# The three passes of a split float32 product in another order

## The chip, the core and the metric

One core of one Trainium2 chip runs the whole program. The metric is the device time of an execution in microseconds; before the change three runs took 2352.8, 2357.6 and 2357.88 us, median 2357.6 us. What is asked is how the reordering of the passes moves this number.

## What is computed

Two blocks on 512 tokens of 1024 features. The first is a hybrid layer, the second a two-layer block with 256 further context tokens:

```python
def hybrid_layer(x, ...):
    h = rmsnorm(x, norm1_w)
    aq, ak, av, bq, bk, bv, br, ba, cq, ck, cv = jnp.split(h @ w_in, ...)
    mix = concat([dilated_attention(aq, ak, av), gla(bq, bk, bv, br, ba), moba_attention(cq, ck, cv)])
    x = x + mix @ w_out
    h2 = rmsnorm(x, norm2_w)
    return x + jnp.square(jax.nn.relu(h2 @ w_ff1)) @ w_ff2
```

The second block (two layers) modulates its norms by a condition vector, projects the input (1024 x 1696), runs latent attention with rotary keys over tokens and context, a Fourier mix and a long convolution, multiplies the mix by an output matrix, and closes each layer with a feed-forward of the same kind (1024 to 4096 and back). All of it is float32, and most of the work is products of a weight matrix with the tokens.

## The kernel before

TensorE takes its operands in the type float32r, which keeps fewer bits than float32. So that a product has float32 accuracy, each operand is split into a high part (the value rounded to float32r) and a low part (the rest), and the product is made of three matmuls into one PSUM bank: high weights on high data, low weights on high data, high weights on low data. `mm3` (L128 to L131) issues these three; in it `whi` and `wlo` are the stationary operand, `xhi` and `xlo` stream. Each matmul comes with a load of its stationary tile, which the profile shows on a row of its own (PEld).

Who makes the four operands: `load_w` (L109 to L119) brings a weight tile of 128 x 1024 by DMA on SP's queue into one of three buffers, ACT writes the high half (`whi`, L117), and DVE subtracts to get the low half (`wlo`, L118). Data are split in the same way by `split` (L133 to L143) or, in the feed-forward, by L261 (ACT, `uh`) and L262 (DVE, `ul`): high on ACT first, low on DVE after it.

Who calls `mm3`: the projections of the first block (`proj1`, 24 passes per weight tile of 128 output features: 8 blocks of 128 input features by three), the scores of its heads and of the second block's attention (there "weights" are the queries and "data" the keys), the projections of the second block (`front`), the heads' queries and keys, the output projections (`out_pieces`), and both halves of the three feed-forwards (`mlp`). The feed-forward goes in 8 groups of 4 hidden tiles: four products with `w1` (24 passes each), the activation on ACT and DVE, then 8 products with `w2` (12 passes each). Behind a norm the first three weight tiles go through one part of the tokens (256 columns) after the other, so that three products are open at once. `values` (L651 to L653), the first block's values (L978 to L980) and the filters (L429) write their three matmuls out by hand and do not use `mm3`.

Order: the program text hands instructions with priorities to a scheduler, which writes each engine's list at build. It takes from what its own estimate says is ready, earliest priority first; matmuls into one bank stay in their order. While the first block's feed-forward runs, work that does not depend on it (modulations, filters, the context's first layer) is handed in on a lane of its own and fills in between; its sums lie in the bank named `e`, the main work's mostly in `d`. From tile 28 of that feed-forward on, the scheduler works with a finer estimate: `timed.enter_context(tc.block(name="second", schedule_with_timeline_sim=True))`.

Of the kernel before, what the change touches and what calls it, by code (L numbers as in the profile page):

```python
# [18 lines left out]
DRAM = bass.MemoryType.DRAM  # L19
# [9 lines left out]
# the parts that the tokens of a stream (0: x, 1: context) are worked on in where a norm would hold up the rest  # L29
# [17 lines left out]
def kernel(ctx: ExitStack, tc: tile.TileContext, A, out, dbg=None):  # L47
# [36 lines left out]
    # ---------------------------------------------------------------- helpers  # L84

    # Buffers of one name are handed out in program order. Work that shall overtake other work needs its own: a lane.
# [34 lines left out]
    def after(cur, prev):  # L121
        """cur is issued behind prev on the same engine."""
        if prev is not None:
            tc.add_manual_dep(cur.ins, prev.ins.name, mybir.DependencyInfo(
                mybir.DependencyClass.NoSync, mybir.DependencyReason.DATA), reason="psum group order")
        return cur

    def mm3(ps, whi, wlo, xhi, xlo, start, stop):  # L128
        pe.matmul(ps, lhsT=whi, rhs=xhi, start=start, stop=False)  # L129
        pe.matmul(ps, lhsT=wlo, rhs=xhi, start=False, stop=False)  # L130
        pe.matmul(ps, lhsT=whi, rhs=xlo, start=False, stop=stop)  # L131

    def split(hi, lo, src, scale=None, shift=None):  # L133
        """hi + lo = src * scale + shift, each exact in float32r."""
# [16 lines left out]
    def rstd_steps(srcs, n, width, psum, name="n", parts=None, gains=None, ending=1):  # L151
        """In two pieces, the steps for the first sources and a call for the rest and the result:
        1 / sqrt(mean over features + eps), on every partition; srcs: [128, n] feature tiles. With parts: a list of
        calls, one per part of the tokens, that give it. With gains: of y = rms_norm(src) * gain, rms_norm(y) being
        src * gain times what the first such list gives, and y src * gain times what the second gives."""
# [18 lines left out]
        def rest():  # L174
            for sl in parts:
                for i in range(together, len(srcs)):
                    add(i, sl)
                if gains:
                    # 1 / (r1 r2)^2 = mean((x gain)^2) + eps / r1^2
# [26 lines left out]
    def normed(hT, srcs, rstd, scale, shift=None):  # L206
        """hT[k] (hi, lo) = srcs[k] * rstd * scale[k] (+ shift[k])"""
# [5 lines left out]
    def normed_stream(hT, v, psum, gain, shift, ending, rest=None):  # L213
        """normed for a whole stream, one part of its tokens after the other"""
# [5 lines left out]
    def by_parts(n_tiles, units, lead):  # L220
        """Order of work of weight tiles on units of tokens: the first tiles go through unit after unit, so that
        later units can still be on their way."""
# [3 lines left out]
    def mlp(streams, w1, w2, pool_u, psum, side=None, rstd=None, ending=1):  # L226
        """x[m] += gate(m) * (relu(h @ w1)^2 @ w2)[m] for each stream (x, hT, n, gate); h = hT (* rstd)"""
        parts = [PARTS[0 if st[2] == S else 1] for st in streams]
        for g in range(32 // GRP):
# [34 lines left out]
            # towards the end the tokens' parts come one after the other, for the norm behind  # L264
# [6 lines left out]
            for mb, mm, ci, sl in steps:  # L271
                if mb not in ws:
                    # the last weights have buffers of their own: the others are for what comes next
# [18 lines left out]
    # ---------------------------------------------------------------- residual streams  # L292
    # The first block needs its input for its first norm and again where it adds to it; in between, the memory
    # of the residual stream serves the modulations.
# [3 lines left out]
    # ---------------------------------------------------------------- work on the second block's weights alone  # L298
# [3 lines left out]
    def filling(behind=0):  # L302
        """Work for when nothing else is ready."""
# [5 lines left out]
    # shift1, norm1_g * (1 + scale1), gate1, shift2, norm2_g * (1 + scale2), gate2; one column per feature tile  # L309
# [5 lines left out]
    def modulations(held, passing, scratch, behind=None):  # L315
        """silu(c) @ w_mod + b_mod for both condition vectors, by products and sums along the free axis."""
# [42 lines left out]
    def filters(fp, psum, which):  # L359
        """Spectra of the long convolutions at the odd half frequencies, cosine and sine parts."""  # L360
# [78 lines left out]
    # ---------------------------------------------------------------- second block, one stream at a time  # L439
# [10 lines left out]
    def mixers(lq, n):  # L450
        """Fourier input, convolution gate, convolution input"""
        return [[lq.tile([128, n], F32, name=f"{nm}{i}") for i in range(2)] for nm in ("F", "x0_", "z")]

    def front_norm(pi, ps, l, v, rest=None):
        """Normed and modulated input."""
# [18 lines left out]
    def front(pi, ps, l, v, lat, mixin, hT):  # L474
        """The input's projections and their latents."""
# [13 lines left out]
        # the convolution's inputs come last: until then their tiles are free  # L489
# [35 lines left out]
        def conv(i, p, dst):  # L525
            """dst = short convolution of channel tile i along tokens"""
# [113 lines left out]
    def values(ap_, ps, l, key_lats):  # L640
        """Values of all heads, token-major."""
# [17 lines left out]
    def attention(ap_, sm, l, v, key_lats, lat, ps, es=None, lp=None, fill=()):  # L659
        """Latent attention of stream v over the keys of key_lats; its output, transposed, in four tiles, which may  # L660
        take the memory of the latents in lp. fill: pieces of other work on the tensor engine."""
# [5 lines left out]
        # the rotary rows of the keys are the same for every head  # L667
# [9 lines left out]
        def heads(j, ps):  # L677
            """queries and keys of a pair of heads"""
# [88 lines left out]
        # behind the rest of the attention in order: for when nothing of it is ready  # L767
# [6 lines left out]
    def out_half(l, half, src, v, ps):  # L774
        """x += gate * (four of the mix tiles) @ w_out"""
# [3 lines left out]
    def out_pieces(l, half, src, v, ending=4):  # L779
        """out_half in pieces, each with the pool of its sums' bank; those of the last weight tiles one part of the  # L780
        tokens after the other"""
# [26 lines left out]
    def side_lane(wrk, width=0, stage=0, split_=0, banks=3):  # L808
        """A lane of its own, with weight buffers where width is given."""
# [704 lines left out]
```

## Time and profile before

| what | value |
|---|---|
| median of three runs | 2357.6 us |
| the profiled execution: span from its first to its last instruction | 2353.3 us |
| TensorE matmul (PE) busy, matmuls | 2287.6 us, 12,907 |
| weight loads (PEld) busy | 1898.1 us |
| VectorE (DVE) busy | 1469.5 us |
| ScalarE (ACT) busy | 996.0 us |
| mean granted TensorE clock | 0.990 |

The profile comes from one execution; the profiled one's time as a run is not listed, only its span, which is 4.3 us below the median of the runs. PE's busy time counts a matmul from its start to a modelled end, and neighbours overlap, so the pace of passes is read from their starts, not from their lengths. `PEld` runs beside `PE`. A wait names what ended an engine's idle time. L-numbers are lines of the kernel.

### The profile page before, as it was taken

How to read it: one execution, taken by the hardware profiler on the slowest of the kernel's cores; microseconds unless marked ns; L12 is line 12 of the kernel's file. 1: busy time of each engine (PE TensorE's matmuls, PEld its weight loads, DVE VectorE, ACT ScalarE, POOL GpSimd, SP SyncE). 2: the span in 40 equal slices, each digit the busy share in tenths (PEclk: the TensorE clock that was granted, in tenths of full speed). 3: DMA queues.
4: the chain of work that ended last, by engine and by line, in shares of the span. 5: the costliest groups of instructions: out<-in, count | busy, mean ns of one | idle time of the engine just before them, and what ended most of it. 6: DMA issues, size and time to landing. Idle time of an engine off the chain costs nothing.

```text
span 2353.3 us, 32927 instructions
## 1 busy us (share of the span) xinstructions
PE 2287.6 (97%) x12907; PEld 1898.1 (81%) x12907; DVE 1469.5 (62%) x2641; ACT 996.0 (42%) x1717; POOL 137.0 (6%) x173
## 2 busy tenths in 40 slices
PE   8999999999999999899999999999899999999997
PEld 7866677778877788788988888888878788888886
DVE  7888778576666684766785554533755666443345
ACT  5344553344344452654533322343443644333333
POOL 0022200000000000321000000000001220000000
PEclk9999999999999999999999999999999999999999
DMA  6523454434331422102354442321222101332232
GB/s 232 166 76 131 130 166 151 164 134 141 126 100 63 149 82 72 54 19 75 106 180 152 152 152 72 103 90 59 83 89 73 41 28 46 107 99 98 90 99 72
DMA packets 78853, 248.52 MB, mean 106 GB/s; under 512 B 9342, under 2 KB 13872, under 8 KB 77930
## 3 DMA queue, kind: packets, MB, share of 16 engines
q1 hardware_dynamic: 78698, 246.42, 31.9%
q8 instruction: 102, 1.67, 0.3%
q14 instruction: 53, 0.43, 0.1%
HBM read 241.63 MB, written 4.75 MB: 105 GB/s over the span
## 4 chain that ended last, share of the span: by engine, by line
PE 87%; DVE 6%; DMA 3%; ACT 2%; issue 1%; POOL 0%; SPq 0%; DVEq 0%; ACTq 0%; POOLq 0%
PE d L129 23%; PE d L130 22%; PE d L131 22%; PE o L760 3%; PE t L750 2%; DVE wlo L118 1%; PE s L129 1%; PE s L131 1%; DMA area<-in_wmod_dram 1%; PE e L129 1%; PE s L130 1%; PE e L429 1%; PE o L1042 1%; PE e L130 1%; PE e L131 1%
## 5 line engine op out<-in xcount | busy, mean ns | idle before, releaser
L117 ACT ACTIVATE whi<-wstage 128x1024 fp32r<-128x1024 f32 (+4 forms) x318 | 324.6, 1024 | 511.0 <-PE d L131 426.3
L118 DVE TENSOR_TENSOR wlo<-wstage,whi 128x1024 fp32r<-128x1024 f32 (+4 forms) x318 | 378.0, 1191 | 256.2 <-ACT whi L117 253.5
L129 PE MATMUL d<-uh,whi 128*128 128x512 f32 (+1 forms) x1056 | 380.4, 361 | 1.3 <-ACT uh L261 1.3
L130 PE MATMUL d<-uh,wlo 128*128 128x512 f32 (+1 forms) x1056 | 379.8, 360 | 0.0
L131 PE MATMUL d<-ul,whi 128*128 128x512 f32 (+1 forms) x1056 | 374.3, 359 | 0.0
L129 PEld LDWEIGHTS d<-uh,whi 128*128 128x128 f32 x1056 | 198.5, 188 | 33.8 <-ACT uh L261 2.2
L131 PEld LDWEIGHTS d<-ul,whi 128*128 128x128 f32 x1056 | 198.9, 188 | 32.4 <-issue 1.5
L130 PEld LDWEIGHTS d<-uh,wlo 128*128 128x128 f32 x1056 | 198.7, 188 | 30.9 <-issue 1.3
L287 DVE SCALAR_TENSOR_TENSOR area<-d,mod,area 128x512 f32<-128x512 f32 (+1 forms) x134 | 95.4, 725 | 145.2 <-PE d L131 145.1
L256 ACT ACTIVATE w<-d 128x256 f32<-128x256 f32 (+1 forms) x96 | 50.4, 525 | 215.9 <-PE d L131 209.2
L338 DVE SCALAR_TENSOR_TENSOR w<-wm,cb 128x1024 bf16<-128x1024 f32 x96 | 114.9, 1220 | 25.7 <-DMA wm<-in_wmod_dram 25.5
L262 DVE TENSOR_TENSOR ul<-w,uh 128x512 fp32r<-128x512 f32 (+1 forms) x128 | 79.3, 622 | 19.9 <-ACT uh L261 19.8
L338 DVE SCALAR_TENSOR_TENSOR mj<-area,area 128x1024 bf16<-128x1024 f32 x64 | 79.7, 1246 | 6.9 <-DMA area<-in_wmod_dram 6.1
L739 DVE TENSOR_REDUCE mx<-s 128x1 f32<-128x768 f32 x64 | 61.2, 956 | 33.6 <-PE s L131 32.8
L260 ACT ACTIVATE w<-w 128x512 f32<-128x512 f32 (+1 forms) x128 | 73.0, 570 | 6.5 <-DVE w L258 5.6
L261 ACT ACTIVATE uh<-w 128x512 fp32r<-128x512 f32 (+1 forms) x128 | 73.9, 577 | 3.5
L744 POOL TENSOR_SCALAR sb<-sb,mx 128x768 f32<-128x768 f32 x64 | 57.9, 906 | 207.7 <-DVE mx L740 80.4
L760 PE MATMUL o<-pt,V 128*64 128x128 f32 x768 | 64.9, 281 | 0.0
L285 DVE TENSOR_TENSOR area<-d,area 128x512 f32<-128x512 f32 (+1 forms) x66 | 44.2, 672 | 31.4 <-PE d L131 31.1
L750 PE MATMUL t<-c_ident,sb 128*128 128x128 f32 x384 | 60.7, 281 | 0.8 <-ACT pt L753 0.7
L674 POOL CAST k000h<-kr0h 32x512 fp32r<-32x512 f32 x2 | 1.7, 844 | 1017.9 <-PE d L625 1017.9
L287 DVE SCALAR_TENSOR_TENSOR ctx<-d,mod,ctx 128x256 f32<-128x256 f32 x64 | 30.8, 481 | 48.0 <-PE d L131 47.8
(1185 smaller groups left out, 5761.0 us busy)
## 6 DMA issues: line engine op xcount, KB each, us to landing
wstage<-in_w_m_dram SPq DMA_DIRECT2D x128, 512.0 KB, 3.5
wstage<-in_w_ff_dram SPq DMA_DIRECT2D x64, 512.0 KB, 4.2
wm<-in_wmod_dram SPq DMA_DIRECT2D x64, 512.0 KB, 4.2
wstage<-in_w_in_dram SPq DMA_DIRECT2D x56, 512.0 KB, 3.4
area<-in_wmod_dram SPq DMA_DIRECT2D x32, 512.0 KB, 4.2
wstage<-in_w_out_dram SPq DMA_DIRECT2D x32, 512.0 KB, 3.5
wstage<-in_w_v_dram SPq DMA_DIRECT2D x8, 520.0 KB, 4.2
ktab<-in_kt_dram SPq DMA_DIRECT2D x16, 256.0 KB, 2.7
```

Of the source, the lines that this page charges most:

```text
L117: act.activation(hi[:, a:b], st[:, a:b], AF.Copy)
L118: dve.tensor_sub(lo[:, a:b], st[:, a:b], hi[:, a:b].bitcast(F32))
L129: pe.matmul(ps, lhsT=whi, rhs=xhi, start=start, stop=False)
L130: pe.matmul(ps, lhsT=wlo, rhs=xhi, start=False, stop=False)
L131: pe.matmul(ps, lhsT=whi, rhs=xlo, start=False, stop=stop)
L260: act.activation(u, r, AF.Square)
L261: act.activation(uh, u, AF.Copy)
L262: mark[g, j] = dve.tensor_sub(ul, u, uh.bitcast(F32))
L287: dve.scalar_tensor_tensor(x[m][:, sl], ps, gate(m), x[m][:, sl], op0=OP.mult, op1=OP.add)
L338: after(dve.scalar_tensor_tensor(t, w, 1.0, sv[v], op0=OP.mult, op1=OP.mult, accum_out=mraw[l][v][j // 8][:, j % 8:j % 8 + 1]), behind)
L750: pe.transpose(pt[:, (kk - a) * 128:(kk - a + 1) * 128], sb[:, kk * 128:(kk + 1) * 128], ident)
L760: last_[h2] = after(pe.matmul(po[64 * h2:64 * h2 + 64, q], lhsT=V[kk][:, 64 * h_:64 * h_ + 64], rhs=PT[h2][:, kk * 128:(kk + 1) * 128], st ...
```

## The change

The second and third pass of `mm3` change places. The rest of the diff takes away comments and descriptions, line for line, so that all line numbers stay.

```diff
     def mm3(ps, whi, wlo, xhi, xlo, start, stop):
         pe.matmul(ps, lhsT=whi, rhs=xhi, start=start, stop=False)
-        pe.matmul(ps, lhsT=wlo, rhs=xhi, start=False, stop=False)
-        pe.matmul(ps, lhsT=whi, rhs=xlo, start=False, stop=stop)
+        pe.matmul(ps, lhsT=whi, rhs=xlo, start=False, stop=False)
+        pe.matmul(ps, lhsT=wlo, rhs=xhi, start=False, stop=stop)
```

## Rows read from the trace of the kernel before

**Rows 1.** Page, part 1: busy time, share of the span, instructions, of each engine.

```profile
PE 2287.6 (97%) x12907; PEld 1898.1 (81%) x12907; DVE 1469.5 (62%) x2641; ACT 996.0 (42%) x1717; POOL 137.0 (6%) x173
```

**Rows 2.** Page, part 4: the chain that ended last, shares by engine.

```profile
PE 87%; DVE 6%; DMA 3%; ACT 2%; issue 1%; POOL 0%; SPq 0%; DVEq 0%; ACTq 0%; POOLq 0%
```

**Rows 3.** Page, part 5: groups; busy us, mean ns | idle before, releaser.

```profile
L117 ACT ACTIVATE whi<-wstage 128x1024 fp32r<-128x1024 f32 (+4 forms) x318 | 324.6, 1024 | 511.0 <-PE d L131 426.3
...
L118 DVE TENSOR_TENSOR wlo<-wstage,whi 128x1024 fp32r<-128x1024 f32 (+4 forms) x318 | 378.0, 1191 | 256.2 <-ACT whi L117 253.5
...
L129 PE MATMUL d<-uh,whi 128*128 128x512 f32 (+1 forms) x1056 | 380.4, 361 | 1.3 <-ACT uh L261 1.3
...
L130 PEld LDWEIGHTS d<-uh,wlo 128*128 128x128 f32 x1056 | 198.7, 188 | 30.9 <-issue 1.3
```

**Rows 4.** Busy time by stretch, PE: length, busy (matmuls), granted clock, DMA, GB/s; last layer.

```profile
2000.00:2100.00 100.00, 100.00 (x435) 1.00 0.33 106
2100.00:2200.00 100.00, 100.00 (x434) 1.00 0.29 95
```

**Rows 5.** Timeline, PE then PEld, 1796 us: start, us, instruction, tiles, shape, count.

```profile
1796.60 0.39 PE L651 MATMUL d<-whi,ckv00h 128*128 128x512 f32 x1
1796.83 0.40 PE L652 MATMUL d<-wlo,ckv00h 128*128 128x512 f32 x1
...
1796.37 0.19 PEld L651 LDWEIGHTS d<-whi,ckv00h 128*128 128x128 f32 x1
1796.61 0.19 PEld L652 LDWEIGHTS d<-wlo,ckv00h 128*128 128x128 f32 x1
```

**Rows 6.** Waits of PE: who, for whom, us in total, times, longest us.

```profile
PE d L130 <- DVE wlo L118: 1.0, 3, 0.4
```

**Rows 7.** Waits of PEld: the same columns.

```profile
PEld d L130 <- DVE wlo L118: 2.3, 4, 0.9
...
PEld e L130 <- DVE wlo L118: 1.2, 7, 0.3
```

**Rows 8.** Timeline, PE, the second weight tile of the start.

```profile
16.11 0.40 PE L129 MATMUL d<-mix0h,whi 128*128 128x512 f32 x1
16.95 0.50 PE L130 MATMUL d<-mix0h,wlo 128*128 128x512 f32 x1 [0.44 <-DVE wlo L118]
```

**Rows 9.** Timeline, PE, first product behind the norm of the first feed-forward.

```profile
313.16 0.28 PE L130 MATMUL d<-h0h,wlo 128*128 128x256 f32 x1
313.49 0.39 PE L131 MATMUL d<-h0l,whi 128*128 128x256 f32 x1
```

**Rows 10.** Timeline, PE, the first feed-forward's first passage from w1 to w2.

```profile
342.69 0.40 PE L129 MATMUL d<-uh,whi 128*128 128x512 f32 x1
343.04 0.50 PE L131 MATMUL d<-ul,whi 128*128 128x512 f32 x1
```

**Rows 11.** Timeline, PE, behind the context's norm in the second block.

```profile
1675.77 0.38 PE L129 MATMUL d<-h10h,whi 128*128 128x256 f32 x1 [0.24 <-ACT h10h L136]
...
1676.46 0.28 PE L130 MATMUL d<-h10h,wlo 128*64 128x256 f32 x1
1677.54 0.58 PE L131 MATMUL d<-h10l,whi 128*128 128x256 f32 x1 [0.81 <-DVE h10l L137]
...
1683.63 0.27 PE L129 MATMUL d<-h14h,whi 128*128 128x256 f32 x1
...
1685.48 0.28 PE L130 MATMUL d<-h15h,wlo 128*64 128x256 f32 x1
```

**Rows 12.** Timeline, DVE then PE, a passage from w1 to w2, last layer.

```profile
2052.09 0.69 DVE L262 TENSOR_TENSOR ul<-w,uh 128x512 fp32r<-128x512 f32 x1
...
2052.84 0.39 PE L130 MATMUL d<-uh,wlo 128*128 128x512 f32 x1
```

**Rows 13.** Stretch, PE, behind the wait of rows 11: the columns of rows 4.

```profile
1677.90:1683.40 5.50, 5.50 (x27) 0.50 0.00 0
```

## What I expect of the change, and why

> **What bounds the kernel now.** I read the page first. TensorE is busy for 2287.6 of 2353.3 us, the next engine (DVE) for 62% [rows 1], and the chain that ended last is PE for 87% of the span [rows 2]. The reader is to see there that PE's list of passes sets the time: only 65.7 us (2353.3 - 2287.6) are left in which PE has nothing running, and most of what a change can do off PE is hidden. The groups come next. One pass of `mm3` has a matmul and a weight load; the load takes 188 ns on its own row, beside the matmul that runs [rows 3]. ACT needs 1.02 us and DVE 1.19 us to split a weight tile in two, and both idle before it until PE has freed a buffer [rows 3]: on the whole weights wait for PE, not PE for weights. In the last layer 434 or 435 matmuls of 512 columns run in 100 us at full clock, so a pass costs 100/434 = 0.230 us [rows 4]; of 256 columns, 16 passes from 1683.63 to 1685.48 us take 1.85 us, 0.116 us each [rows 11]. Then I read the waits of PE and of its loads for the two operands that change places, the low weights and the low data [rows 6, 7], and last the timeline where each of them is made just in time [rows 8 to 12], and the clock behind the longest such hole [rows 13].
>
> **What the change does to a triple.** The first pass stays. The pass that reads the low data (`xhi`'s remainder) becomes the second, the pass that reads the low weights becomes the third. No pass, load, split or DMA is added or removed, and the sum in PSUM ends with the third pass as before, so whoever empties the bank waits for the same number of passes. What moves are four deadlines, each by one pass: low weights may come 0.230 us later (0.116 us at 256 columns), low data must come as much earlier; the high weights and the low data are let go one pass earlier, the low weights and the high data one pass later.
>
> **The passes themselves: 0, ends -5 and +5 us.** 12,907 matmuls [rows 1] before and after. Which tile streams while which one is loaded does change, and no row of before shows the new pairs in `mm3`. The spread between like stretches, 434 against 435 passes [rows 4], is 0.23%, about 5 us on the span; I keep it as the bound on both sides and take 0, because the nearest row with the new pairing is plain. In `values` the stationary tile is already used twice in a row (`ckv00h` in L651 and L652), and there the second pass starts 0.23 us after the first, like any other [rows 5].
>
> **The repeated high weights: 0.** After the change the first and second pass of each triple have the same stationary tile. In the same rows it is loaded again, 0.19 us at 1796.37 and 0.19 us at 1796.61 us [rows 5]: the second load is not left out, and it lies beside a running matmul either way. At 256 columns, where a load has less to hide behind, a pass still costs 0.116 us, half of the 0.230 us of 512 columns; so the loads do not set the pace there either, and leaving one out would win at most 0.0004 us on a third of 12,907 passes, 2 us. The Trainium skill, "TensorE: Matmul & The Clock Gate", Part 2, says that loading is decoupled from computing so that one can load once and matmul repeatedly, which speaks for this order. Here the trace does not agree that it happens by itself: the tile is loaded twice. By the rule one load in three would go; by the rows that gives 0 to 2 us, so the sum is the same.
>
> **Low weights later: -1.0 us, ends 0 and -1.8 us.** PE waits for `wlo` in the second pass 3 times, 1.0 us in all [rows 6]; its loads wait 4 times in the main stream (2.3 us) and 7 times in the filling work (1.2 us) [rows 7]. Each such wait can shrink by one pass at most: 4 x 0.230 + 7 x 0.116 = 1.7, rounded up to 1.8. An example is the second tile of the start: first pass at 16.11 us, second only at 16.95 us, because the low weights are late [rows 8]; now the low-data pass fits into that hole. Some of the seven lie in filling work for which something else stands ready, so I take 1.0.
>
> **Low data earlier: +1.5 us, ends +0.8 and +6.8 us.** This is where the change costs. Behind a norm or an activation the high half comes from ACT and the low half from DVE after it, and PE so far bridges that with the low-weight pass of every product that is open. Behind the norm of the first feed-forward two products are open, and PE waits from 313.16 + 0.12 to 313.49 us for `h0l` [rows 9]: two passes fewer to fill with, 2 x 0.116 = 0.23. Behind the context's norm three are open (six passes from 1675.77 us, the last at 1676.46), then PE stands until 1677.54 us for `h10l`, 0.81 us of it idle [rows 11]: 3 x 0.116 = 0.35. In the first passage from w1 to w2 two products are open and `ul` comes some 0.1 us late already (342.69 + 0.23 against 343.04) [rows 10]: one pass more, 0.23. The other 23 passages (8 groups in each of three feed-forwards, less this one) have room by the planner's order: in the last layer `ul` is done at 2052.09 + 0.69 = 2052.78 us, and the slot that will want it starts at 2052.84 [rows 12]. 0.06 us is little, but nothing is lost; I take 0 and keep 23 x 0.23 = 5.3 for the upper end. About five more norm edges and six head pairs make up a guess of 0.7 (five to six times one pass of 0.116). 0.23 + 0.35 + 0.23 + 0.7 = 1.5.
>
> **Releases: 0.** High weights freed a pass earlier and low weights a pass later: ACT splits first and DVE follows 1.02 us behind it [rows 3], so the later release of 0.23 us is not the last to come; if that cover went, it would cost 0.23 us where a tile is waited for, which is inside the ends above. SP's and POOL's queues have nothing moved past them.
>
> **The order that is written at build.** The program's list on each engine is laid out by a scheduler that takes what is ready by its own estimate. Its estimate of `wlo` and `ul` now falls in other slots, so pieces of filling work can land elsewhere. The trace cannot show the new list. The unit of such a mishap is one product, 24 passes x 0.230 = 5.5 us, put into a stretch where PE would idle, or taken out of one; I take 0 and let it make the rivals.
>
> **Sum.** -1.0 + 1.5 = +0.5 us. It is made against the profiled span, 2353.3 us; the median of the runs is 2357.6, so 4.3 us lie around the span, and I leave them as they are: 2357.6 + 0.5 = 2358.1 us. The direct ends alone are -1.0 (0.8 - 1.8) and +6.8; with the pass rate's 5 us they are 2351.6 and 2369.4 us.
>
> **Rivals.** (A) Slower: the low data become the late operand. Place: the passages from w1 to w2. If `ul` is not there at the second pass in all 24, they cost 5.3 us more than I count: 2363.4 us. It decides where the slack at today's third pass is under one pass, 0.23 us; for it speaks that the slack in rows 12 is 0.06 us after the change, against it that the scheduler has other banks open to fill with, as rows 10 show (another product's first pass at 342.69). A hole can also cost clock: behind that of rows 11 the granted clock is 0.50, the lower of the two levels (1.2 GHz), for 5.5 us with 27 passes [rows 13], 0.20 us each against 0.116 from 1683.63 on [rows 11]; 5.5 - 27 x 0.116 = 2.4 us. One more such stretch makes 2366. (B) Faster: the new list happens to put one or two products into today's 65.7 us without matmuls: -5.5 to -11 us, about 2350. For it speaks only that the idle time is there; against it that most of it lies at the start, at the norms and at the end, where nothing is ready. The same with the other sign, 2364 us or so, is as likely by itself. (C) Faster: the second load of the same tile does not happen after all; by the rows above 2 us at most, 2356, which is within the forecast. (D) The pairs of streamed and loaded tiles are better or worse by the whole spread of rows 4: 2353 or 2363.
>
> **How the numbers follow.** About 0.2%, 4.7 us, is what a measurement of this kernel can tell from no change. Forecast (with C): 0.51. Slower: A 0.19, the list 0.07, D 0.03, together 0.29. Faster: B 0.16, D 0.04, together 0.20. I take the range from 2348 to 2369 us: it holds the direct ends with the pass rate, one product won or two lost, and leaves out the rest of B and the worst of A with several slow-clock stretches.
>
> **What would show it.** Right: matmuls 12,907 and loads as many; passes of 0.230 us in the last layer; PE's waits for `wlo` nearly gone and waits for `ul`, `h..l` new, in the second pass; the wait for `h10l` near 1.2 instead of 0.81 us. The prediction is wrong if the pace of passes in the last layer differs from 434 in 100 us by more than one, if passages from w1 to w2 show PE idle in every group, or if the stretches with filling work end earlier or later by several microseconds with no wait that answers for it.

## The result, and the profile after

The changed kernel takes 2370.17 us (four runs, 2365.75 to 2373.19) against 2357.74 us: a ratio of 1.0053 [1.0038, 1.0067], or 12.4 us more. Measured once more beside other kernels it took 2369.99 us, 1.0052 [1.0035, 1.0069]. The prediction, 2358.1 us with a range up to 2369, was wrong: the change costs time, and it costs more than any rival had priced.

The page of the profile after (span 2363.7 us, mean granted clock 0.987), with the lines that answer to [rows 1 to 3]: part 1, the shares of the chain from part 4, groups of part 5.

```profile
PE 2296.7 (97%) x12907; PEld 1901.7 (80%) x12907; DVE 1472.8 (62%) x2641; ACT 1003.2 (42%) x1717; POOL 136.2 (6%) x173
...
PE 87%; DVE 6%; DMA 3%; ACT 2%; issue 1%; POOL 0%; SPq 0%; DVEq 0%; ACTq 0%; POOLq 0%
...
L117 ACT ACTIVATE whi<-wstage 128x1024 fp32r<-128x1024 f32 (+4 forms) x318 | 325.7, 1027 | 797.8 <-PE d L130 678.4
...
L130 PEld LDWEIGHTS d<-ul,whi 128*128 128x128 f32 x1056 | 198.9, 188 | 32.8 <-issue 1.7
...
L131 PEld LDWEIGHTS d<-uh,wlo 128*128 128x128 f32 x1056 | 198.5, 188 | 31.7 <-issue 1.7
```

The reader is to see that nothing in kind has changed: as many matmuls, as many loads, those of the feed-forwards at the same 188 ns, the same chain. L130 is now the pass of the low data, L131 that of the low weights. Nor does PE stand still much longer: its idle time was 2353.3 - 2287.6 = 65.7 us and is 2363.7 - 2296.7 = 67.0 us. Its busy time grew by 9.1 us, so the same passes took longer. What is different stands in three other views. First the pace in the last layer (busy time by stretch, PE: length, busy, matmuls, granted clock, DMA, GB/s), 432 where [rows 4] had 434:

```profile
2020.00:2120.00 100.00, 100.00 (x432) 1.00 0.30 95
2120.00:2220.00 100.00, 100.00 (x432) 1.00 0.30 96
```

Second PE's waits (who, for whom, us in total, times, longest us) and those of its loads; compare [rows 6, 7]:

```profile
PE t L1035 <- POOL sb L1032: 4.3, 5, 1.3
...
PE d L129 <- ACT h0h L139: 1.5, 1, 1.5
...
PE d L130 <- DVE h10l L137: 1.1, 1, 1.1
...
PE d L130 <- DVE h0l L140: 0.7, 1, 0.7
...
PE d L131 <- DVE wlo L118: 0.7, 2, 0.4
...
PE d L130 <- DVE h00l L137: 0.4, 1, 0.4
...
PE e L131 <- DVE wlo L118: 0.2, 1, 0.2
...
PEld e L131 <- DVE wlo L118: 2.2, 8, 0.4
...
PEld d L131 <- DVE wlo L118: 1.3, 2, 0.7
```

Between 85 and 335 us the trace of before has 3.2 us for the first of these lines and 0.8 for the second:

```profile
PE t L1035 <- POOL sb L1032: 3.2, 6, 1.0
...
PE d L129 <- ACT h0h L139: 0.8, 1, 0.8
```

Third, the granted clock behind these gaps (the columns of the first view), after and then before:

```profile
208.90:212.30 3.40, 2.17 (x12) 1.00 0.33 129
212.30:215.70 3.40, 3.40 (x11) 0.50 0.00 0
...
236.20:239.60 3.40, 2.32 (x10) 1.00 0.37 134
239.60:243.00 3.40, 3.40 (x11) 0.50 0.05 20
314.70:318.10 3.40, 1.39 (x9) 1.00 1.02 300
318.10:321.50 3.40, 3.40 (x18) 0.51 1.04 291
```

```profile
208.90:212.30 3.40, 3.40 (x27) 1.00 0.49 178
212.30:215.70 3.40, 3.24 (x18) 1.00 0.40 118
...
236.20:239.60 3.40, 2.40 (x11) 1.00 0.76 258
239.60:243.00 3.40, 3.40 (x20) 1.00 0.07 27
314.00:317.40 3.40, 3.40 (x30) 1.00 1.07 228
317.40:320.80 3.40, 3.40 (x26) 1.00 0.55 164
```

After the change PE stands still for 1.2 us at 209.6 and again at 236 (a transpose waits for the softmax that POOL finishes) and for 1.5 and 0.7 us at the norm of the first feed-forward, and behind each the granted clock is 0.50, the lower of its two levels (1.2 GHz). In the profile of before none of these three falls is there. A profile is one execution, so the falls from 200 to 330 us are counted over all traces of the runs below, without the two kernels that were filled in block 1 (here the first block up to its output projection). With the new order in block 1's head scores all six traces have one to three falls there. With the old order seven of eight have none. One, of the kernel with low weights first in the last feed-forward, has one at 237.7 us, behind a wait of 1.0 us at which the kernel before, with the same list of passes up to there, kept its clock.

To see where the time lies I take the ends of the same eight DVE instructions in each trace (the first `ul`, the 33rd and 64th maximum of L739, the 1st, 127th, 145th and 181st sum of L287, the end) and list how much longer each stretch is than in the profile of before. In brackets stands half of what its stretches at half clock are longer: the work that the clock withheld.

| us, from before | to 330 | to 1023 | to 1150 | to 1668 | to 1883 | to 2070 | to 2282 | to the end | sum |
|---|---|---|---|---|---|---|---|---|---|
| changed | +5.1 (+5.1) | +0.8 | +1.1 | +0.3 | -0.2 (+1.7) | +2.0 (+1.7) | +1.3 | 0.0 | +10.4 (+8.6) |
| changed, again | +12.7 (+13.7) | 0.0 | +1.0 | +0.3 | -0.2 (+1.7) | +1.9 (+1.7) | +1.3 | 0.0 | +17.0 (+17.1) |

Two things can be read. The large, varying part lies before 330 us, and there it is the size of the lost clock. A steadier part of 4 to 5 us lies behind it, 1.3 us of it in 212 us of the last feed-forward where PE never waits and the clock is 1.00. The Trainium skill, "TensorE: Matmul & The Clock Gate", Terms, prices time at the half clock at one half of it. Up to 330 us the two traces agree (5.1 for 5.1, 12.7 for 13.7); later the price is lower. From 283 us on two kernels of the last section, with block 1's heads or its projections taken back, have the changed kernel's list of passes. From 1668 to 1883 us these four traces took -1.3, -0.2, -0.2 and +1.0 us against before, with 0, 1.7, 1.7 and 3.4 us of work withheld: 2.3 us for 3.4, about two thirds.

### The profile page after: what moved, and what is told of

Read it like the earlier page. It is cut to its first block, busy times and chain, and to the rows that moved or that the text cites. A ratio compares the mean times of both kernels' runs of the same rounds, so it can differ in the third digit from the quotient of the medians.

```text
span 2363.7 us, 32973 instructions
## 1 busy us (share of the span) xinstructions
PE 2296.7 (97%) x12907; PEld 1901.7 (80%) x12907; DVE 1472.8 (62%) x2641; ACT 1003.2 (42%) x1717; POOL 136.2 (6%) x173
## 4 chain that ended last, share of the span: by engine, by line
PE 87%; DVE 6%; DMA 3%; ACT 2%; issue 1%; POOL 0%; SPq 0%; DVEq 0%; ACTq 0%; POOLq 0%
PE d L130 22%; PE d L129 22%; PE d L131 22%; PE o L760 3%; PE t L750 2%; DVE wlo L118 1%; PE s L129 1%; PE s L131 1%; PE s L130 1%; PE e L129 1%; DMA area<-in_wmod_dram 1%; PE o L1042 1%; PE e L131 1%; PE e L130 1%; ACT whi L117 1%
## 5 line engine op out<-in xcount | busy, mean ns | idle before, releaser
L130 PE MATMUL d<-ul,whi 128*128 128x512 f32 (+1 forms) x1056 | 378.8, 360 | 0.0
L131 PE MATMUL d<-uh,wlo 128*128 128x512 f32 (+1 forms) x1056 | 378.4, 360 | 0.0
L129 PE MATMUL d<-uh,whi 128*128 128x512 f32 (+1 forms) x1056 | 375.6, 360 | 1.0 <-ACT uh L261 1.0
L130 PEld LDWEIGHTS d<-ul,whi 128*128 128x128 f32 x1056 | 198.9, 188 | 32.8 <-issue 1.7
L129 PEld LDWEIGHTS d<-uh,whi 128*128 128x128 f32 x1056 | 198.6, 188 | 32.6 <-ACT uh L261 1.7
L131 PEld LDWEIGHTS d<-uh,wlo 128*128 128x128 f32 x1056 | 198.5, 188 | 31.7 <-issue 1.7
L287 DVE SCALAR_TENSOR_TENSOR area<-d,mod,area 128x512 f32<-128x512 f32 (+1 forms) x134 | 95.5, 725 | 151.9 <-PE d L131 151.1
L739 DVE TENSOR_REDUCE mx<-s 128x1 f32<-128x768 f32 x64 | 61.2, 956 | 35.3 <-PE s L131 34.5
L753 ACT ACTIVATE pt<-t 128x384 f32<-128x384 f32 x64 | 31.3, 489 | 74.0 <-PE t L750 73.7
L742 ACT ACTIVATE sb<-s,mx 128x768 f32<-128x768 f32 x64 | 57.3, 896 | 4.2 <-DVE mx L740 4.0
```

The lines of the kernel that those rows point to most:

```text
L130: pe.matmul(ps, lhsT=whi, rhs=xlo, start=False, stop=False)
L131: pe.matmul(ps, lhsT=wlo, rhs=xhi, start=False, stop=stop)
L287: dve.scalar_tensor_tensor(x[m][:, sl], ps, gate(m), x[m][:, sl], op0=OP.mult, op1=OP.add)
```

## The experiments

In the kernels below that mix the orders, `mm3` has a switch, so that each call can take either order; off is the order of before. Times of one comparison stand beside runs of the kernel before on the same chip; those had medians of 2356.7 to 2359.06 us, so the ratios are what counts.

**Halves of the change.** The new order in all three feed-forwards alone, everywhere else alone, in the last feed-forward alone, and in block 1 (projections, head scores, way out) alone:

```diff
-    def mm3(ps, whi, wlo, xhi, xlo, start, stop):
+    def mm3(ps, whi, wlo, xhi, xlo, start, stop, new=False):
...
-                    mm3(..., uh[:, sl], ul[:, sl], k == 0, k == GRP - 1)
+                    mm3(..., uh[:, sl], ul[:, sl], k == 0, k == GRP - 1, True)
```

> New order in all three feed-forwards and nowhere else; the list is that of before up to 300 us. Theory C: a half-clock stretch at 318 us (first norm) and a longer one at 1987 us, +3.4 us, those at 212 and 240 us absent. Theory P: about 1600 triples of 512 columns at +2 to +3 ns, +3 to +5 us, spread evenly over the feed-forwards. Theory D: up to 24 passages of 0.23 us, +5.5 us, in waits of PE for ul.

> The complement: new order everywhere but in the feed-forwards. Theory C: the half-clock stretches at 212 and 240 us and those in the attention stretches (950 to 985, 1816 to 1840 us), together about +5 us, 2363 us; pace in the last layer 434 in 100 us. Theory P: about 400 triples, +1.2 us. Theory D: +1 us.

> New order only in the feed-forward of the last layer; PE's list is that of before up to its norm (about 1980 us), so every microsecond of difference arises in the last 370 us. Theory P (the pace of passes depends on which tile streams while which is loaded): 432 instead of 434 matmuls in 100 us, about +1.5 us from 2010 us to the end with no new waits of PE in that stretch. Theory C (holes behind late data lower the granted clock): one more half-clock stretch at the norm before it, 3.4 us long, +1.7 us, and nothing after. Theory D (low data late at the 8 passages from w1 to w2): 434 in 100 us as before and 8 new waits for ul of about 0.2 us, +1.8 us.

> New order only in the first block's projections, head scores and output projection; there PE's list is that of the changed kernel. Theory C: the half-clock stretches at 212 and 240 us, which the changed kernel has and the one before has not, come back: about +3.4 us by 330 us, granted clock near 0.988, 2361 us. Theory P: some 400 triples of 512 columns at +3 ns, +1.2 us. Theory D: a few waits for low data, +0.5 us.

The last two columns split the span (mean over the runs): span times granted clock, that is what it would have been at full clock, and the rest, which the clock withheld.

| new order in | us | ratio | mean clock | at full clock | withheld |
|---|---|---|---|---|---|
| nothing (before, 31 runs) | 2356.8 | 1 | 0.9886 | 2328.2 | 26.9 |
| feed-forwards | 2361.3 | 1.0017 [1.0006, 1.0028] | 0.9878 | 2329.9 | 28.8 |
| all but these | 2361.05 | 1.0019 [1.0010, 1.0029] | 0.9866 | 2327.9 | 31.6 |
| last feed-forward | 2361.27 | 1.0016 [1.0006, 1.0026] | 0.9877 | 2329.8 | 29.0 |
| block 1 | 2360.84 | 1.0019 [1.0009, 1.0028] | 0.9862 | 2326.8 | 32.6 |

Each piece costs about 4 us, and as far as intervals of 2 to 3 us to either side can tell, what pieces contain of each other does not add: the last feed-forward alone costs what all three do, block 1 what all but the feed-forwards do. Two costs of different kinds come out. The feed-forwards cost about 2 us at full clock, where pace belongs, and about 2 in clock; block 1 keeps its pace, and all its cost is clock. Theory D fell: in none of the four traces does PE wait for `ul`. Theory C's stretches came in part: block 1 alone shows one fall, at 237 us, where two were expected, and the feed-forwards alone none at 318 us. The pace of the last layer, with the new order there (last feed-forward only) and without it (all but the feed-forwards):

```profile
2120.00:2220.00 100.00, 100.00 (x432) 1.00 0.30 95
```

```profile
2120.00:2220.00 100.00, 100.00 (x434) 1.00 0.29 95
```

From 2070 to 2282 us each of the eight traces with the new order in the last feed-forward shows 1.3 us more than before, and each of those with the old order there 0.0. From 2020 to 2320 us the mean distance of the starts of two passes is 231.1 ns in the old order and 232.2 to 232.4 ns in the new one; for some 1500 passes that is 1.7 us. But alone the halves make 3.6 and 4.3 us by the means of their runs, 7.9 together, where the changed kernel's mean is 12.1 above that of before.

**The change once more, and two further orders for the pace.** One run each of the last feed-forward with low weights first (2354.75 us) and with low data first (2361.66 us); single runs, so their times are not compared, only their pace:

```diff
+        a, b, c = ((wlo, xhi), (whi, xhi), (whi, xlo)) if new else ((whi, xhi), (wlo, xhi), (whi, xlo))   # low weights first
+        a, b, c = ((whi, xlo), (whi, xhi), (wlo, xhi)) if new else ((whi, xhi), (wlo, xhi), (whi, xlo))   # or: low data first
+        for i, (w_, x_) in enumerate((a, b, c)): pe.matmul(ps, lhsT=w_, rhs=x_, start=start and i == 0, stop=stop and i == 2)
```

> The changed kernel once more, on the chip and in the company of the kernels below. Measured so far: 2370.17 us against 2357.74 us of the kernel before, 1.0053 [1.0038, 1.0067], but with four runs of each; the two halves of the change (feed-forwards alone 1.0017, all else 1.0019) add up to 1.0036 only, that is some 2365.3 us beside 2356.8 us. If the halves add, this gives a ratio of 1.0030 to 1.0042; if they act on each other (one half's later edges falling into the other's), 1.0046 to 1.0060. Clock theory: the excess over the kernel before is for the most part in the share of the span at half clock, so that span times granted clock, as a mean over the runs, lies within 3 us of the 2328.2 us of the kernel before, and span times (1 - clock) 4 to 8 us above its 27. Pace theory (passes dearer in the new order): span times clock lies 5 us or more above it.

> The kernel before, with another order of the three passes in the last layer's feed-forward alone: low weights on high data, high weights on high data, high weights on low data. In the changed order this stretch runs 432 passes of 512 columns per 100 us instead of 434. Theory S (each change of the streamed data tile costs some 3 ns: two changes per three passes before, three in the changed order): here there are two changes, so 434 per 100 us. Theory W (the second of two neighbouring passes with one weight tile costs more, since its load finds the same tile in use): here two neighbouring passes share the high weights, as in the changed order, so 432. Three passes at the last layer's pace: 691.2 ns at 434, 694.4 ns at 432.

> The kernel before, with a further order of the three passes in the last layer's feed-forward alone: high weights on low data, high weights on high data, low weights on high data. Theory S (changes of the streamed tile: two per three passes, as before): 434 passes of 512 columns per 100 us. Theory W (neighbouring passes with one weight tile, as in the changed order): 432. A third possibility, that the place of the low data in the middle of the three decides: 434, and with theory S it would be told apart only by an order with low data in the middle.

The change came out as before: 1.0052, in the range that was set for halves that act on each other, though its interval, [1.0035, 1.0069], reaches into that for halves that add. By means it is 4.2 us more than the halves' sum, with a standard error of 1.7: they probably act on each other, and how is open. Neither theory of that expectation holds alone. In these four runs span times clock is 2332.2 us, 4.0 above before, where the clock theory allowed 3 and the pace theory wanted 5; what the clock withheld is 35.5 us, 8.5 above 27, where 4 to 8 was expected. Low weights first (first fence) and low data first (second):

```profile
2120.00:2220.00 100.00, 100.00 (x433) 1.00 0.29 94
2220.00:2320.00 100.00, 100.00 (x434) 1.00 0.28 91
```

```profile
2120.00:2220.00 100.00, 100.00 (x432) 1.00 0.30 94
2220.00:2320.00 100.00, 100.00 (x432) 1.00 0.28 94
```

In mean distances these are 231.8 and 232.2 ns. Theory S wanted 434 for both and is out, the third possibility with it (low data are not in the middle here, and 432 came). Theory W (the second of two neighbouring passes with one weight tile is slower) fits the count of low data first, but the starts of the passes speak against it. In the last feed-forward (2020 to 2320 us, some 400 of each step, without steps of 260 ns and more) the old order takes 232.2 ns to the second pass, 232.1 to the third and 229.0 to the next three's first; the new one 231.6, 231.9 and 232.9. The step onto the repeated high weights (231.6) is no slower than those within the old three. What is lost is the short step from the old third pass to the next three. The order sets the pace, by up to 0.5%; why that one step is short is not settled.

**Filling the gaps, before the change.** If gaps bring the low clock, work in the gaps should keep it up. Products that nothing reads were put behind the sums of the norms on the main path (72 calls, 144 more matmuls):

```diff
                 pe.matmul(ps, lhsT=ones, rhs=acc[:, sl], start=True, stop=True)
+                keep = WARM and warm and sl.start == 0 and bank(psum)   # WARM = (8, 4)
-                return newton(ps, m, width, acc[:, sl] if ending > SP else None)
+                for _ in range(WARM[0] if keep else 0): pe.matmul(keep[:, :m], lhsT=ones, rhs=acc[:, sl], start=True, stop=True)
+                r = newton(ps, m, width, acc[:, sl] if ending > SP else None)
+                for _ in range(WARM[1] if keep else 0): pe.matmul(keep[:, :m], lhsT=ones, rhs=r, start=True, stop=True)
+                return r
```

> The kernel before with its order of passes, and with matrix products that nothing reads put into the gaps of the norms on the main path: 8 of the ones tile with the norm's sums behind the product that the norm needs, 4 with the finished reciprocal root, of 256 columns or fewer, into a spare bank; so TensorE has work where it stood still for 1 to 1.5 us at each. Clock theory (an idle gap at a norm is followed by a stretch at half clock, and that is what the time of these kernels varies with): the stretches at about 823, 1677 and 1981 us, 13.7 us long in sum before, shrink or vanish, and the time falls by 2 to 6 us, to 2351 to 2355 us, although TensorE does more. Rival (the gaps themselves are the cost and the clock follows the load of the whole span): the stretches stay, the added products (about 12 at 0.12 us at each norm) lie in the gaps or behind them, and the time stays or rises by up to 5 us, 2357 to 2362 us.

The time was 2371.68 us, 1.0062 [1.0047, 1.0077], a miss for both theories, by 17 us for the clock theory's 2351 to 2355. The clock itself did what the clock theory says: it rose from 0.9884 to 0.9922 in the mean, and the three falls named are gone (17.1 us long in sum before, not the 13.7 of the expectation). Before and, at the places that answer to them, filled:

```profile
820.00:840.00 20.00, 17.01 (x111) 0.83 0.29 110
1670.00:1700.00 30.00, 23.91 (x160) 0.89 0.25 82
1970.00:2000.00 30.00, 26.02 (x199) 0.94 0.12 36
```

```profile
820.00:840.00 20.00, 19.25 (x124) 1.00 0.30 112
1685.00:1715.00 30.00, 28.43 (x210) 1.00 0.25 88
1985.00:2015.00 30.00, 30.00 (x225) 1.00 0.14 52
```

But I had priced a product at 0.12 us; it is two matmuls of 0.216 us each, 144 x 0.216 = 31 us in all, far more than the gaps hold, and at two of the norms (1097 and 1125 us) PE had other work. At full clock the spans are 23 us longer than before, and the clock withheld 9 us less. So a smaller filling was made, for both orders: 38 matmuls, 8.2 us, at the four gaps alone (block 1's decay, a factor of its gated linear attention, and three norms).

```diff
+                if keep and sl.start == 0 and acc is accs[-1]: warm(psum, acc[:, sl], keep)   # keep: 4, 5, 6 by norm
+        warm(ps1, e[:, :256], 2, "t")      # behind the exponent of block 1's decay
         act.activation(l, e, AF.Ln, bias=1.0)
+        warm(ps1, l[:, :256], 2, "t")
```

> The kernel before with its order of passes and a smaller filling than the one that cost 14 us: products that nothing reads, at 0.216 us each (16 of them took 3.46 us there), only where the trace of before shows TensorE standing still for 1.8 to 3.1 us ahead of a stretch at half clock: 8 at the first block's decay (gap of 2.37 us at 89.6), 8 between the two sums of the norm at 821, 10 and 12 behind the first sum of the norms at 1671 and 1975. Clock theory: the stretches at about 823, 1677 and 1981 us (13.7 us in sum in the profile of before, 6.8 us more of each at half clock than at full for every 13.7) go, the one at 93 may shrink, nothing else moves: 2348 to 2354 us, span times (1 - clock) at 16 to 22 instead of 27. Rival (the load decides, the gaps do not): the stretches stay and the time is 2356 to 2359 us.

> The changed kernel with the same filling. Clock theory: it loses the same stretches, with the one at 1987 us being 6.8 us long in its profiles instead of 3.4, so that it gains 3 to 9 us over the changed kernel, to 2361 to 2367 us; it stays above the filled kernel before by what its stretches between 212 and 321 us and the slower pace of the last layer (432 passes of 512 columns per 100 us instead of 434, 1.7 us) cost, 7 to 13 us. Rival (the changed order costs time by itself, whatever the clock): no gain, 2368 to 2372 us.

Before, filled: 2368.98 us, 1.0049 [1.0033, 1.0064], a miss for both theories. After, filled: 2367.0 us, 1.0044 [1.0029, 1.0059], at the upper end of the clock theory's 2361 to 2367, but it was to stay 7 to 13 us above the filled kernel before and came out 2 us below it, so that half missed. The mean clock is 0.9910 instead of 0.985, and by the ratios it gained 2 us on the changed kernel, whose interval overlaps: the clock gave back 13.6 us, and the spans at full clock grew by 11.8. The trace of the filled kernel before shows where it lost (PE's wait for the softmax, which is now L1040, then two gaps in it and what follows):

```profile
PE t L1040 <- POOL sb L1037: 4.9, 6, 1.5
```

```profile
212.80:216.20 3.40, 1.93 (x18) 1.00 0.06 23
216.20:219.60 3.40, 3.40 (x10) 0.51 0.49 154
...
243.60:247.00 3.40, 2.28 (x12) 1.00 0.32 83
247.00:250.40 3.40, 3.40 (x11) 0.50 0.18 74
```

The products at the decay moved the later list, the waits in block 1's heads grew from 3.2 to 4.9 us, and two falls of the clock came in the very place where the changed kernel has them, with the old order of passes. By 330 us it is 9.6 us behind, 8.5 of it clock. That is the mechanism without the change. From 1668 to 2070 us, though, it spends 6.8 us less at half clock than before, 3.4 us of work, and is 0.1 us slower: there 22 of the products stand, 4.8 us of passes, so this run cannot tell whether the stretches cost nothing or the filling ate what it won. Over the whole program its four runs have the mean clock of before (0.9880 against 0.9879); what block 1 lost in clock the rest won back, and the 11 us that it is slower lie at full clock, near the 8.2 us of products put in. No filled kernel beats the kernel before.

**Block 1's calls taken back or done alone.** The head scores, as one example:

```diff
-                        mm3(p[:, c], qp[0][r, q], qp[1][r, q], kp[0][r, c], kp[1][r, c], True, True)
+                        mm3(p[:, c], qp[0][r, q], qp[1][r, q], kp[0][r, c], kp[1][r, c], True, True, False)
```

> The changed kernel with one call of the three passes back in the old order: the head scores of block 1, whose softmax the transposes of line 1035 wait for. In the changed kernel TensorE waits 4.3 us there between 85 and 335 us, at most 1.3 us at once, against 3.2 and 1.0 us before, and in its profiles the clock then stands at 0.50 in stretches between 212 and 277 us that the kernel before does not show. Theory H (these gaps bring the stretches, the stretches the time): the wait is back at 3.0 to 3.3 us, no half clock between 200 and 300 us, and the time falls by 3 to 6 us, from 2370 to 2364 to 2367 us. Rival N (the gap at the norm at 313 us, or the clock at random, costs the time): the time stays at 2369 to 2371 us, or falls by the 1.1 us of the gaps alone.

> The kernel before with the new order in one call alone: the head scores of block 1. Theory H: PE's wait for POOL at line 1035 rises from 3.2 to about 4.3 us, a stretch at half clock stands between 205 and 277 us, and the time rises by 3 to 5 us to 2360 to 2362 us, the whole of what block 1's three calls together cost (2361.5 us as a mean). Rival N: the time rises by 0 to 1 us, to 2357 to 2358 us, with the clock there at 1.00.

> The changed kernel with all three calls of block 1 (its projections, its head scores, its way out) back in the old order; feed-forwards and both layers stay in the new one. Sum theory: two parts that do not depend on each other. One is order alone: up to 2 us at each feed-forward, and in the last one 1.3 us between its 144th and 180th sum, found in each kernel with the new order there and in no other; from 355 us to the end this came to about 5 us in the three traces of kernels with the full new order from there on. The other is TensorE's clock before 330 us, 5.1 to 13.7 us in two profiles of the changed kernel. This kernel keeps the first and loses the second: 2361.5 to 2363.5 us. Rival (all of it is the clock, and it falls as often without block 1's change): 2366 to 2370 us. Second rival (block 1's calls cost only what they cost alone, 4.1 us): 2366 us.

> The changed kernel with block 1's projections alone back in the old order; its head scores, whose softmax TensorE waits for, keep the new one. With the heads alone changed, that wait was 3.8 us (1.2 at most) and the time that of the kernel before; with projections and heads changed it was 4.3 us (1.3) and the time 3.9 us longer at least. Theory I (the two act together: the projections' passes are what TensorE has left to do while the softmax runs): the wait is at 3.8 us or less, and the time falls by 3 to 6 us, to 2364 to 2367 us, as with the heads alone taken back. Rival (the heads' own order decides): 4.3 us, 2369 to 2371 us.

In this table the idle time of PE is 130 us less its busy time from 200 to 330 us; the waits are those from 85 to 335 us.

| order: heads / projections / way out / feed-forwards and layers | us | ratio | PE idle, 200 to 330 | clock there | wait for softmax | waits for `h0h` + `h0l` |
|---|---|---|---|---|---|---|
| old / old / old / old (before) | 2357.74 | 1 | 2.9 | 1.00 | 3.2 | 0.8 |
| old / old / old / new | 2361.65 | 1.0017 [1.0006, 1.0028] | 3.1 | 1.00 | 3.1 | 0.8 + 0.3 |
| new / old / old / old | 2357.98 | 0.9999 [0.9990, 1.0009] | 4.1 | 0.99 | 3.8 | 0.8 |
| old / new / new / new | 2364.85 | 1.0034 [1.0022, 1.0046] | 4.2 | 1.00 | 3.2 | 1.5 + 0.7 |
| new / old / new / new | 2364.16 | 1.0023 [1.0012, 1.0033] | 5.5 | 0.97 | 3.9 | 1.5 + 0.7 |
| new / new / new / old | 2360.84 | 1.0019 [1.0009, 1.0028] | 5.5 | 0.97 | 4.3 | 1.5 + 0.3 |
| new / new / new / new (changed) | 2370.17 | 1.0053 [1.0038, 1.0067] | 5.9 | 0.96, 0.93 | 4.3 | 1.5 + 0.7 |

The rows of three of them, in the order of the table: block 1 old, heads old, changed.

```profile
200.00:330.00 130.00, 126.92 (x729) 1.00 0.47 146
```

```profile
200.00:330.00 130.00, 125.85 (x698) 1.00 0.45 142
```

```profile
200.00:330.00 130.00, 124.09 (x668) 0.96 0.43 134
```

With block 1 taken back the kernel came to 2361.65 us, in the 2361.5 to 2363.5 that the sum theory gave, and its mean clock, 0.9884, is that of the kernel before: the 4 us that it still costs are not clock. The split of the spans shows the two parts. At full clock they are 2327.9 us before (70 runs), 2332.8 changed (eight runs) and 2332.7 with block 1 taken back; withheld by the clock are 27.7, 34.9 and 27.4 us. So in the changed kernel block 1's order costs 7 to 8 us, all of it clock, and the order behind block 1 costs 4 to 5 us at full clock. Done alone, block 1 cost 4 us; the other 4 are part of what the halves do to each other. Heads taken back: wait back at 3.2, no half clock between 200 and 300 us, 2364.85 us, as theory H said. Heads alone: the wait rose to 3.8 us, not to 4.3, one fall came, and no time was lost, so theory H fails as it stood: the heads' order alone is not enough. With the projections taken back instead, the wait was 3.9 us (0.1 above theory I) and the time 2364.16 us, inside theory I's 2364 to 2367. So the heads cost nothing in the kernel before and about 4 us on top of the rest of the change; the projections and the way out cost about 4 us without the heads (2364.85 against 2361.65, by ratios 1.0034 against 1.0017). The table gives the idle time and the clock of one execution each; they go together in the main, not call by call (idle 4.2 at 1.00, 4.1 at 0.99).

**The clock as a cause of the spread.** Sorted by their mean granted clock, the 70 runs of the kernel before average 2361.5 us at 0.986, 2359.2 at 0.987, 2357.8 at 0.988, 2357.4 at 0.989, 2355.0 at 0.990 and 2353.1 at 0.991. Within each kernel's own runs (164 in all) a thousandth of clock goes with 1.36 us (standard error 0.09); withheld work alone would be 0.001 x 2360 = 2.36. The changed kernel's eight runs lie 0.0030 lower than before, 4.1 us by the runs and 7.1 by the withheld work; the rest of its 12.4, 5 to 8 us, holds the 4 to 5 of the order. The longer gaps themselves (4.3 - 3.2, and 1.5 + 0.7 - 0.8, about 2.5 us) are hardly seen in the sum: PE's idle time in all rose by 1.3 us.

## Why the prediction was wrong, step by step

- **The passes themselves, 0 with ends -5 and +5.** Failed, within its ends: the last feed-forward runs 432 in 100 us, the bound at which the prediction called itself wrong, and rival D had named the case. I took the pace from `values` [rows 5], where the repeated tile is the same but the third pass is not; what changed is the step behind the third pass, from 229.0 to 232.9 ns. Up to 1.8 us. (100/434 = 0.230 counts passes that lie partly outside the stretch; by starts a pass was 0.231 us.)
- **The repeated high weights, 0.** Held: 12,907 loads, those of the feed-forwards 188 ns each as before, no load left out. The trace agrees with the rows and not with the rule weighed there (the Trainium skill, "TensorE: Matmul & The Clock Gate", Part 2, one load for several matmuls): it does not come true by itself.
- **Low weights later, -1.0.** Failed: nothing was won. PE's waits fell from 1.0 to 0.9 us (0.7 + 0.2), and its loads' waits stayed at 3.5 (2.3 + 1.2 before, 1.3 + 2.2 after): they went from the main stream into the filling work. The upper end, 0, was right.
- **Low data earlier, +1.5.** Right at two places: `h10l` went from 0.81 to 1.1 us (1.16 was worked out), and no passage from w1 to w2 shows PE waiting for `ul`, so the 23 passages cost the 0 that was taken. The 0.23 for the first passage did not come either (its wait, for `uh`, went from 1.3 to 1.0 us). Too small at the first feed-forward's norm: `h0l` 0.7 us where 0.3 was worked out (0.1 before and 0.23 more), and `h0h` rose by 0.7, which no step held: it is 1.5 us in each kernel of the last table whose way out, the product ahead of that norm, has the new order, and 0.8 in the others.
- **The head scores, in a guess of 0.7 with five norms.** This is the step that failed most. The guess names eleven places and prices five or six, at 0.116 us each, and nothing for the clock. No row of the prediction is from block 1 between 113 and 271 us, where PE waits for POOL's softmax; its wait grew by 1.1 us, and behind the gaps the clock fell. In the changed kernel block 1's order costs 7 to 8 us, all of it clock.
- **The order written at build, 0.** The doubt was right in part: 1.1 us from 1023 to 1150 us have no wait that answers for them. But no stretch of the table shows a product won or lost (5.5 us); what grew were the gaps in block 1 and the clock behind them.
- **The clock.** It stood in a rival only, as one more stretch at 2.4 us, and at nothing in the sum. The profile of the changed kernel has 17 us more at half clock, 8.6 us of work. The prediction took the clock as a price on a gap already found; it did not ask which gaps would be the next.
- **The base.** In the 70 runs of the kernel before the time is 2.07 to 2.25 us above the span, so the profiled execution stands for a run of about 2355.5 us; the 4.3 us that the prediction laid around the span were half of them the spread of the runs, which goes with the clock.

Of the rivals, A had the sign and the clock, but its place, the passages from w1 to w2, shows nothing.

## What to carry to other kernels

Where one engine is busy for 97% of the span, look for its gaps before its work: a reordering that adds a microsecond to gaps of the busiest engine can cost several, by the clock behind them. List each place where that engine already waits (here the waits of 0.8 us at the first norm and of up to 1.0 us in the heads grew into waits with falls behind them), and ask of a change what it takes out of the work that stood behind the wait; costs of two such changes need not add. Filling gaps with idle work is no way out by itself: it kept the clock up at the gaps it filled and still lost, by the work that it put in and by the list that it moved.

## What the runs showed of the hardware

- The order of three passes with the same operands sets the pace of float32r matmuls of 512 columns: 231.1, 231.8, 232.2 and 232.3 ns in four orders in the last feed-forward, the same within 0.2 ns in each kernel with that order (1.3 us in 212 us, in eight traces of eight). In the middle feed-forward (1150 to 1660 us) three passes took 694.4 ns before and 696.7 after. In the first, from 300 to 500 us, they took 693.3 and 693.7: there the step onto the repeated high weights is the short one (229.9 ns), in place of the step behind the third pass (230.2 before, 231.6 after). Why is open.
- The falls of the clock are not fixed for one list. Up to 95 us PE's list is the same in the kernel before and in eight of those here, and the fall at the gap at 89.6 us (waiting for block 1's decay) was 3.4, 6.8, 10.2 or 13.7 us long in their profiles, in three of them in two pieces of 3.4; in the two profiles of the changed kernel it was 6.8 and 17.1 us (granted clock from 85 to 115 us 0.89 and 0.72). That alone is up to 5 us of withheld work between runs, beside a spread of 2352 to 2362 us.
- Time at half clock costs nearly what it withholds up to 330 us (5.1 us for 5.1 and 12.7 for 13.7), two thirds of it from 1668 to 1883 us (2.3 us for 3.4, four traces of one list), and 1.36 us for 2.36 withheld over all runs.
- Not settled: why the stretch from 1023 to 1150 us takes 1.1 us longer with the new order in the feed-forward behind it, with no wait that answers for it; and why the halves of the change cost more together than apart.
